# Last feed-forward block: the third group's down projection by seven block products, and the closing norm by quarters of a set

## Chip, core and metric

The kernel runs on one core of a Trainium2 chip. The metric is the device time of one execution in microseconds, as the median of several runs. TensorE is written PE, its weight loads PEld, VectorE DVE, ScalarE ACT, GpSimd POOL and SyncE SP; SP and POOL issue nearly all transfers.

## What is computed

Two encoder layers (a feed-forward block, a token mixer, a second feed-forward block) over 512 tokens and 16 meta tokens, 1024 channels wide, and a closing norm. The part that matters here is the second feed-forward block of the second layer and the norm behind it:

```python
def rmsnorm(x, g):
    xf = x.astype(jnp.float32)
    y = xf * lax.rsqrt(jnp.mean(xf * xf, axis=-1, keepdims=True) + EPS)
    return (y * g.astype(jnp.float32)).astype(x.dtype)

def swiglu(x, w_gate, w_up, w_down):
    return (jax.nn.silu(x @ w_gate) * (x @ w_up)) @ w_down
...
        h = h + 0.5 * swiglu(rmsnorm(h, norm_gains[l, 2]),
                             ffn_w_gate[l, 1], ffn_w_up[l, 1], ffn_w_down[l, 1])
    return rmsnorm(h, final_norm)[:, N_META:]
```

The hidden width is 2816, the model width 1024.

## The kernel before

Channels lie on the 128 partitions, tokens along the free dimension; `hall` holds the 8 channel chunks of `h`. In the last block only the 512 real tokens are live. Every f32 operand is cut into a rounded part (`hi`) and the rest (`lo`), and each product is three matmuls: hi·hi, hi·lo, lo·hi. ACT makes the hi part of a weight block (line 310, tile `whi`), DVE the lo part (line 311, tile `wlo`); both have four buffers.

A feed-forward block is named by layer and place: (0,0), (0,1), (1,0), (1,1). It walks over 11 pairs of hidden chunks in groups of 4, 4 and 3 pairs. For a pair, gate and up come from seven block products instead of eight (a scheme of Strassen's kind): weights and tokens are each cut in two, the seven products "1" to "7" use sums and differences of the blocks (line 621, 24 matmuls of 256 or 264 tokens each). A group's down projection goes by seven block products too where the group is "fast" (`fast_down`, line 745): the 1024 output channels are taken as two sets `dq` of 512, the products of one set have 2 x 3 x n matmuls (n pairs in the group, so 18 in the third group). A set's result has four quarters, two chunks of channels (`m`) by one half of the tokens (`q`). Product "1" alone opens an accumulator X, "6", "7" and "4" are added to it in turn; "2" opens Y; "5" opens Z and "3" is added to it. After each product DVE adds the accumulator to a quarter of `h` (line 753), before the next one may add to the same accumulator. The quarters of a set are finished by "2", "3", "7" and "4".

In blocks (0,0) and (1,0) all three groups are fast; in (0,1) and (1,1) the third is not: its down projection goes chunk by chunk of `h` (`down`, line 488), six hidden chunks for each of eight output chunks, 512 tokens at a time, and for the last three chunks of (1,1) 256 at a time (`ending`, from line 1277): first token half, then second, so that the first half's mean of squares, root and output pieces run beside the second half's products.

Weight blocks that are sums (s3 = 21 - 11, s4, and the sums for "5" and "6") are made by transfers that add into memory in SBUF (`add`, line 224, issued by POOL), by DVE, or by ACT, which negates a block first (lines 219 and 277). Plain blocks are loaded by SP (line 214), slabs of ordinary weights too (line 287). `fetch` runs 9 blocks ahead, `make` 3 or 4 ahead of the product that uses a block.

The order of the instructions on each engine is set by a scheduler from the order of the code and its dependencies; each engine takes its own list in that order. The order of the products of a third fast group is the list `CLOSING`: set 1 "1", 0 "6", 1 "2", 0 "7", 0 "3", 0 "4", 1 "5", 1 "6", 1 "7", 1 "3", 1 "4"; set 0's "1", "5" and "2" stand ahead of it.

Of the kernel before, what the change touches and what calls it, by code (L numbers as in the profile page):

```python
# [39 lines left out]


GROUPS = (4, 4, 3)
ALL_FAST = [(0, 0), (1, 0)]
LAST = [sum(GROUPS[: g + 1]) - 1 for g in range(len(GROUPS))]
QUADS = 2
LATE = 5
# [1 line left out]
OPENING = ((0, 0), 0), ((0, 0), 1)  # L48
AB = (1, 0, 1, 0, 0, 0, 1, 1, 1, 1, 1)
PACE = 0  # L50
CLOSING = tuple(zip((1, 0, 1, 0, 0, 0, 1, 1, 1, 1, 1), "16273456734"))
PLACE = {p: i for i, p in enumerate("1256743")}
DIRECT = {"1": "11", "2": "12", "4": "22"}
# [6 lines left out]
def ffn_steps(f):  # L60
# [3 lines left out]
    for g, n in enumerate(GROUPS):  # L64
# [122 lines left out]
class Weights:  # L187
# [3 lines left out]
    def __init__(self, tc, raw, hi, lo, wts, win):  # L191
# [12 lines left out]
        self.behind = None  # L204
# [45 lines left out]
    def sums(self, f, i, product, w):  # L250
# [44 lines left out]
    def make(self, upto):  # L295
        nc = self.nc
        while self.made < min(upto, len(self.loads)):
# [14 lines left out]
            self.got[s] = (hi, lo)  # L312
            self.got.pop(s - 12, None)
            self.made += 1
            if not isinstance(load, int) and load[2] in "126":
# [36 lines left out]
def build(tc, ctx, xt, wts, win, par, w2, const, umask, out):  # L352
# [243 lines left out]
    def ffn(l, f, norm, done, following):  # L596
# [94 lines left out]
        def operand(g, c, ks=None):  # L691
# [1 line left out]
            ks = ks or slice(0, GROUPS[g])  # L693
            src = raw[g][{"1": 0, "2": 2, "5": 0, "6": 0, "7": 1, "3": 3, "4": 2}[c]]
            if (g, c) not in sets:
                tag = "c" if c in "56" else "g"
# [15 lines left out]
        def operands_of(g, ks, order):  # L712
            for c in order:
                if c == "5":
                    difference(g, 0, 1, 0, ks)
                operand(g, c, ks)

        def operands_behind(g, dq, c):
            if (dq, c) == (1, "1"):
                difference(g, 1, 1, 3)  # L720
                operand(g, "7")
            elif (dq, c) == (1, "2"):
                operand(g, "3")
                difference(g, 2, 2, 0)
                operand(g, "4")

        def fast_down(g, dq, c, part):
# [22 lines left out]
            for m, q in {"1": [(0, 0)], "2": [(0, 0)], "5": [(1, 1)], "6": [(0, 1)], "3": [(0, 1)], "7": [(1, 1)],  # L750
                         "4": [(1, 0)]}[c]:
                to = hall[:, 4 * dq + 2 * m : 4 * dq + 2 * m + 2, q * w : (q + 1) * w]
                V.tensor_tensor(to, to, acc, ALU.add)  # L753
            if g == len(GROUPS) - 1:
# [522 lines left out]
    def finish_chunk(c):  # L1277
        fin.square(c)
        gain(c, slice(0, SEQ))

    def ending(sums, operand, rs):

        table("abs_reciprocal_sqrt_and_small")
# [150 lines left out]
```

## Time and profile before

| | us |
|---|---|
| median of 3 runs (2187.23 to 2188.65) | 2187.77 |
| the profiled execution | 2187.4 |
| its span, first to last instruction | 2185.6 |
| PE busy | 2149.1 (98%) |
| DVE busy | 1802.6 (82%) |
| ACT busy | 1245.9 (57%) |
| POOL busy | 119.0 (5%) |

A row of the chain of waits gives start and length and what ran; a row of the timeline adds, in brackets, the idle time of the engine ahead of it and what ended it. A row of transfers gives tiles, issuing queue, count, size and the time from issue to landing. `x24` counts instructions.

### The profile page before, as it was taken

The numbers are of one execution on the slowest core, as the hardware profiler recorded it, in microseconds if no ns is written. First come the engines' busy times: TensorE is split into PE (matmuls) and PEld (weight loads), VectorE is DVE, ScalarE is ACT, GpSimd is POOL, SyncE is SP. The second block draws the span as 40 slices with busy tenths as digits, with TensorE's granted clock in tenths as the row PEclk, the third lists the DMA queues.
The fourth block names the chain that finished last, engine by engine and source line by source line (L and its number), as shares of the span: only waits on it lengthen the run. The fifth ranks groups of instructions, "written<-read, shape, count | busy, mean of one in ns | idle before, by whom it ended". The sixth has DMA issues, their size and how long they took to land.

```text
span 2185.6 us, 40161 instructions
## 1 busy us (share of the span) xinstructions
PE 2149.1 (98%) x16434; PEld 2056.1 (94%) x16434; DVE 1802.6 (82%) x2751; ACT 1245.9 (57%) x1844; POOL 119.0 (5%) x140
## 2 busy tenths in 40 slices
PE   7999999999999999999999999999999999999998
PEld 7999999989999999999999999988788888999997
DVE  8887979776976689888789979797779767997986
ACT  8545556444784556454575455574557836554544
POOL 1100000000000000010010000000000001000100
PEclk9999999999999999999999999999999999999999
DMA  9866755212113467676567667553121146775751
GB/s 286 218 195 182 202 154 139 82 51 76 49 40 123 130 177 180 202 185 183 167 162 187 199 181 204 153 140 97 49 78 49 49 135 152 199 204 178 196 162 68
DMA packets 91223, 320.32 MB, mean 147 GB/s; under 512 B 10144, under 2 KB 12576, under 8 KB 91040
## 3 DMA queue, kind: packets, MB, share of 16 engines
q1 hardware_dynamic: 70048, 246.58, 33.9%
q0 software_dynamic: 19584, 69.21, 17.6%
q8 instruction: 129, 2.11, 0.4%
q10 hardware_dynamic: 1408, 1.97, 0.3%
q14 instruction: 54, 0.44, 0.1%
HBM read 294.65 MB, written 2.10 MB: 136 GB/s over the span
## 4 chain that ended last, share of the span: by engine, by line
PE 83%; DVE 9%; ACT 4%; DMA 2%; issue 2%; SPq 0%; DVEq 0%; ACTq 0%
PE ss L621 36%; PE mm L488 15%; PE ss L745 14%; PE ss L488 7%; DVE wlo L311 3%; PE sm L488 2%; DMA w<-win 2%; PE sm L1125 1%; PE ss L1100 1%; ACT whi L310 1%; PE ss L494 1%; DVE h L753 1%; PE sm L1141 1%; PE ss L1101 1%; PE sm L1142 1%
## 5 line engine op out<-in xcount | busy, mean ns | idle before, releaser
L621 PE MATMUL ss<-xc,whi 128*128 128x264 f32 (+1 forms) x4928 | 903.1, 285 | 11.3 <-ACT whi L310 7.4
L621 PEld LDWEIGHTS ss<-xc,whi 128*128 128x128 f32 x4928 | 764.5, 189 | 14.9 <-ACT whi L310 8.0
L621 PE MATMUL ss<-xc,wlo 128*128 128x264 f32 (+1 forms) x2464 | 700.6, 285 | 4.0 <-DVE wlo L311 4.0
L311 DVE TENSOR_TENSOR wlo<-w,whi 128x1024 fp32r<-128x1024 f32 (+2 forms) x355 | 423.7, 1200 | 66.7 <-ACT whi L310 66.3
L621 PEld LDWEIGHTS ss<-xc,wlo 128*128 128x128 f32 x2464 | 465.0, 189 | 5.9 <-DVE wlo L311 5.9
L310 ACT CAST whi<-w 128x1024 fp32r<-128x1024 f32 (+2 forms) x355 | 362.1, 1036 | 169.3 <-PE ss L621 80.1
L488 PE MATMUL mm<-x,whi 128*128 128x264 f32 (+1 forms) x1712 | 385.5, 315 | 0.0
L488 PEld LDWEIGHTS mm<-x,whi 128*128 128x128 f32 x1712 | 278.1, 188 | 16.3 <-issue 1.0
L745 PE MATMUL ss<-g,whi 128*128 128x264 f32 (+1 forms) x1520 | 284.3, 285 | 3.6 <-DVE h L753 1.7
L488 PE MATMUL mm<-x,wlo 128*128 128x264 f32 (+1 forms) x856 | 266.3, 316 | 0.0
L745 PEld LDWEIGHTS ss<-g,whi 128*128 128x128 f32 x1520 | 236.2, 188 | 7.5 <-DVE g L706 3.6
L745 PE MATMUL ss<-g,wlo 128*128 128x264 f32 (+1 forms) x760 | 215.2, 283 | 0.0
L625 ACT COPY c<-ss 128x528 f32<-128x528 f32 (+1 forms) x132 | 78.4, 594 | 239.0 <-PE ss L621 238.7
L310 ACT CAST whi<-raw 128x1024 fp32r<-128x1024 f32 x114 | 119.3, 1048 | 130.7 <-PE mm L488 94.2
L311 DVE TENSOR_TENSOR wlo<-raw,whi 128x1024 fp32r<-128x1024 f32 x114 | 139.0, 1220 | 57.2 <-ACT whi L310 53.2
L488 PEld LDWEIGHTS mm<-x,wlo 128*128 128x128 f32 x856 | 159.6, 188 | 8.5 <-issue 0.5
L745 PEld LDWEIGHTS ss<-g,wlo 128*128 128x128 f32 x760 | 143.0, 188 | 0.0
L224 POOL DMA_DIRECT2D w<-win x64 | 56.1, 876 | 1453.2 <-DVE t L1261 342.0
L745 PE MATMUL ss<-c,whi 128*128 128x264 f32 (+1 forms) x608 | 115.5, 285 | 0.3
L311 DVE TENSOR_TENSOR wlo<-s,whi 128x1024 fp32r<-128x1024 f32 (+1 forms) x94 | 112.2, 1195 | 1.6 <-ACT whi L310 1.4
L467 ACT ACTIVATE c<-c 128x528 f32<-128x528 f32 (+1 forms) x88 | 56.5, 642 | 98.5 <-DVE c L671 98.4
L488 PE MATMUL ss<-g,whi 128*128 128x264 f32 (+2 forms) x516 | 103.6, 310 | 0.0
(270 smaller groups left out, 3379.1 us busy)
## 6 DMA issues: line engine op xcount, KB each, us to landing
w<-win SPq DMA_DIRECT2D x333, 512.0 KB, 4.4
raw<-wts SPq DMA_DIRECT2D x114, 512.0 KB, 3.3
w<-win POOLq DMA_DIRECT2D x60, 512.0 KB, 7.5
s<-win POOLq DMA_DIRECT2D x26, 512.0 KB, 7.5
w<-s POOLq DMA_DIRECT2D x26, 512.0 KB, 6.1
w<-win SPq DMA_DIRECT2D x20, 384.0 KB, 3.6
s<-w POOLq DMA_DIRECT2D x8, 512.0 KB, 7.4
h<-xt SPq DMA_DIRECT2D x3, 528.0 KB, 6.0
```

The lines of the kernel that those rows point to most:

```text
L224: self.nc.gpsimd.dma_start(t, src, accum_op=ALU.add)
L310: nc.scalar.copy(hi[:, cs], w[:, cs])
L311: nc.vector.tensor_tensor(lo[:, cs], w[:, cs], hi[:, cs].bitcast(F32), ALU.subtract)
L467: prev_act[0] = S.activation(*args, **kw).ins
L488: TE.matmul(acc.half[i][:width], lhs, rhs[:, acc.spans[i]], start=first, stop=last)
L494: TE.matmul(a, weights, x[:, hs], start=True, stop=True)
L621: TE.matmul(acc[:, j], a[:, j, k], b[:, at], start=bool(begin and k == 0 and i == 0), stop=k == len(x) - 1 and i == 2, skip_group_check=no ...
L625: W.behind = S.copy(part(st, q), acc).ins
L745: closing[0] = TE.matmul(acc[:, j], a[:, j, k], xs[b][:, k], start=bool(begin and k == 0 and i == 0), stop=k == n - 1 and i == 2, skip_gro ...
L753: V.tensor_tensor(to, to, acc, ALU.add)
L1100: TE.matmul(s[:n, i, :HF], lhs, kh[:, hs], start=True, stop=False)
L1101: TE.matmul(s[:n, i, :HF], lhs, kl[:, hs], start=False, stop=True)
```

## The change

Block (1,1) joins the list `ALL_FAST`, so its third group's down projection goes by seven block products for each of the two sets. The order of its last eleven products is a list of its own, `FINAL_CLOSING`. The chunkwise closing of that block (`ending`) is no longer reached; as soon as a quarter of a set is finished, `quarter_done` scales it, squares it, sums the squares per token half and multiplies it with the gain. The second token half's four quarters are finished first; its mean, root and four output pieces are to go while the first half's last quarters are made. One weight sum (the "3" of set 1) is made by DVE from a block that is loaded a second time, instead of by an adding transfer. Of the code:

```diff
-ALL_FAST = [(0, 0), (1, 0)]
+ALL_FAST = [(0, 0), (1, 0), (1, 1)]
...
+FINAL = (DEPTH - 1, 1)
+FINAL_CLOSING = ((1, "1"), (0, "6"), (0, "3"), (1, "6"), (0, "7"), (1, "5"), (1, "7"), (1, "3"), (0, "4"), (1, "2"), (1, "4"))
...
-                    turns = [("S", g, dq, c, 3) for dq, c in CLOSING]
+                    turns = [("S", g, dq, c, 3) for dq, c in (FINAL_CLOSING if f == FINAL else CLOSING)]
...
+        elif product == "5" and self.behind_sum and f == FINAL:
+            s4, s2, key = self.behind_sum
+            V.tensor_tensor(s4, s2, s4, ALU.subtract)
+            got[key], self.behind_sum = s4, None
+        elif product == "6" and f == FINAL and i == NOP - 1:
+            s4 = self.block(f, i, "12", self.long, "wsa")
+            self.behind_sum = s4, w, (f, i, "3")
...
         def operands_behind(g, dq, c):
+            if final(g):
+                if (dq, c) == (1, "1"):
+                    difference(g, 1, 1, 3)
+                    operand(g, "3")
+                    operand(g, "7")
+                    difference(g, 2, 2, 0)
+                elif (dq, c) == (1, "5"):
+                    operand(g, "4")
+                return
...
+            if final(g):
+                if c in "2374":
+                    quarter_done(dq, *{"2": (0, 0), "3": (0, 1), "7": (1, 1), "4": (1, 0)}[c], rs)
...
+    def quarter_done(dq, m, q, rs):
+
+        half = slice(q * SEQ // 2, (q + 1) * SEQ // 2)
+        c = 4 * dq + 2 * m
+        x2 = hall[:, c : c + 2, half]
+        left[q] -= 1
...
+        V.scalar_tensor_tensor(x2, x2, -0.25, rs[:, half].unsqueeze(1).broadcast_to([P, 2, SEQ // 2]), ALU.mult, ALU.mult)
+        sq = v2(slot("t")[:, :SEQ])
+        S.activation(sq, x2, AF.Square)
+        if q not in acc:
+            acc[q] = sq
+        elif left[q] or q:
+            V.tensor_tensor(acc[q], acc[q], sq, ALU.add)
+        for i in range(2):
+            gain(c + i, half)
+        for _ in range(2 if len(waiting) > 2 else 1):
+            if waiting:
+                leave2(*waiting.pop(0))
+        if left[q] == 0:
+            t = pair(q == 1)[:, 0, : SEQ // 2]
+            parts = [acc[q][:, 0], acc[q][:, 1]] + ([sq[:, 0], sq[:, 1]] if q == 0 else [])
+            for i, p in enumerate(parts):
+                TE.matmul(t, o1024, p, start=i == 0, stop=i == len(parts) - 1)
...
+            S.activation(y, t, AF.Abs_reciprocal_sqrt, bias=eps, scale=1.0)
+            S.activation(u, y, AF.Square)
+            V.scalar_tensor_tensor(u, t, EPS, u, ALU.add, ALU.mult)
+            V.scalar_tensor_tensor(y, u, 3.0, y, ALU.subtract, ALU.mult)
...
+    def leave2(q, c, y, n):
+        half = slice(q * SEQ // 2, (q + 1) * SEQ // 2)
+        x2 = hall[:, c : c + n, half]
+        V.scalar_tensor_tensor(x2, x2, -0.5, y.unsqueeze(1).broadcast_to([P, n, SEQ // 2]), ALU.mult, ALU.mult)
+        (S if q == 0 and c % 4 == 0 else nc.sync).dma_start(out[:, c : c + n, half], x2)
```

Up to the last three pairs of this block the lists of all engines stay as they were. Line numbers grow: in the changed kernel hi and lo weight parts are lines 319 and 320, gate and up products 630, fast down products 766, additions to `h` 774.

On ACT, the stretch just ahead of the last group's down products read before (a semaphore named DMASW belongs to a transfer issued by POOL, DMAHW to one by SP):

```order
L310 CAST whi_24674<-raw_24479 128x1024 [waits DMAHW4_49,DVE_49]
L310 CAST whi_24710<-raw_24517 128x1024 [waits DMAHW5_49,PE_49]
L310 CAST whi_24747<-raw_24554 128x1024 [waits DMAHW6_49,DVE_49,PE_49]
L467 ACTIVATE c_24408<-c_24408 128x512 [waits DVE_49]
L310 CAST whi_24751<-raw_24586 128x1024 [waits DMAHW7_49,PE_49,Activation_49]
```

Now this stands there, around the second to fifth of the eleven turns (`w_11_15` and `s_11_15` are weights of set 0, `w_11_16` and `s_11_16` of set 1; 24766 serves (0,"6"), 24827 (0,"3"), 24862 (1,"6"), 24889 (0,"7"); c_24793, g_24853 and g_24857 are the hidden operands of "6", "3" and "7"):

```order
L319 CAST whi_24766<-w_11_15_24413 128x768 [waits DMASW2_49,PE_49]
L319 CAST whi_24827<-s_11_15_24770 128x768 [waits DMASW4_49,PE_49]
L712 CAST c_24793<-g_24277 128x256 [waits DVE_49]
L472 ACT_TABLE_LOAD
L319 CAST whi_24862<-w_11_16_24553 128x768 [waits DMASW6_49,PE_49]
L709 ACTIVATE g_24853<-g_24280 128x768 [waits DVE_49]
L319 CAST whi_24889<-s_11_15_24631 128x768 [waits DMASW0_49,PE_49]
L712 CAST g_24857<-g_24278 128x768 [waits PE_49]
```

The casts of plain loaded slabs have gone; casts of weights that adding transfers make stand among the casts of the operands.

On DVE, the same place held this before:

```order
L684 TENSOR_TENSOR c_24407<-c_24407 128x512
L477 TENSOR_TENSOR g_24742<-c_24407,g_24742 128x512
L311 TENSOR_TENSOR wlo_24781<-raw_24621,whi_24780 128x1024
L587 TENSOR_TENSOR h<-h,ss_24612 128x512
L587 TENSOR_TENSOR h<-h,ss_24661 128x512
```

And now (ss_24693 is set 0's accumulator X, ss_24744 its Z, ss_24765 its Y):

```order
L320 TENSOR_TENSOR wlo_24767<-w_11_15_24413,whi_24766 128x768
L715 TENSOR_TENSOR c_24794<-g_24277,c_24793 128x256
L774 TENSOR_TENSOR h<-h,ss_24693 128x2x256
L774 TENSOR_TENSOR h<-h,ss_24744 128x2x256
L710 SCALAR_TENSOR_TENSOR g_24854<-g_24280,g_24853 128x768
L774 TENSOR_TENSOR h<-h,ss_24765 128x2x256
L715 TENSOR_TENSOR g_24858<-g_24278,g_24857 128x768
L1316 SCALAR_TENSOR_TENSOR h<-h,rs_21346 128x2x256
L320 TENSOR_TENSOR wlo_24828<-s_11_15_24770,whi_24827 128x768
```

The low part of (0,"3")'s weights, the last row, stands behind the operands of "3" and "7", which take their hi parts from ACT.

At the end of PE's list the first half's mean stood between the second half's products before:

```order
L1295 MATMUL ss_24929<-t_24792,const 128x256
L488 MATMUL ss_24856<-g_24314,whi_24747 128x256 x2
L488 MATMUL ss_24856<-g_24314,wlo_24748 128x256
L488 MATMUL ss_24856<-g_24279,whi_24747 128x256 x2
L488 MATMUL ss_24856<-g_24279,wlo_24748 128x256
L488 MATMUL ss_24856<-g_24547,whi_24751 128x256 x2
L488 MATMUL ss_24856<-g_24547,wlo_24752 128x256
L1300 MATMUL ss_24929<-t_24926,const 128x256
```

Now its list ends so (ss_25058 is the second token half's mean, ss_25153 the first's):

```order
L766 MATMUL ss_24826<-c_24997,whi_25066 128x256
L766 MATMUL ss_24826<-c_24996,wlo_25067 128x256
L1332 MATMUL ss_25058<-t_24915,const 128x256 x2
L1332 MATMUL ss_25153<-t_24822,const 128x256 x2
L1332 MATMUL ss_25153<-t_25147,const 128x256 x2
```

Both means stand behind the last product.

More of the change, by code (lines that the diff above doesn't have):

```diff
@@ L203, in __init__ @@
         self.pos = 0
-        self.behind = None
+        self.behind = self.behind_sum = None
     def dram(self, f, i, name):
@@ L314, in make @@
             self.made += 1
-            if not isinstance(load, int) and load[2] in "126":
+            if not isinstance(load, int) and load[2] in "1265":
                 self.sums(*load, w)
@@ L695, in operand @@
             if (g, c) not in sets:
-                tag = "c" if c in "56" else "g"
+                tag = "c" if c in "56" or final(g) and c == "4" else "g"
                 sets[g, c] = [quarter(tag, F32R) for _ in range(2)]
@@ L716, in operands_of, with final @@
                 operand(g, c, ks)
+        def final(g):
+            return done is None and g == len(GROUPS) - 1
         def operands_behind(g, dq, c):
+            if final(g):
[7 more added lines that the diff above has]
+                return
             if (dq, c) == (1, "1"):
@@ L753, in fast_down @@
                 V.tensor_tensor(to, to, acc, ALU.add)
-            if g == len(GROUPS) - 1:
+            if final(g):
+                if c in "2374":
+                    quarter_done(dq, *{"2": (0, 0), "3": (0, 1), "7": (1, 1), "4": (1, 0)}[c], rs)
+            elif g == len(GROUPS) - 1:
                 if c in "34":
@@ L1279, in finish_chunk @@
         gain(c, slice(0, SEQ))
+    left = {0: 4, 1: 4}
+    acc, factor_of, ms_of, waiting = {}, {}, {}, []
+    def quarter_done(dq, m, q, rs):
[3 more added lines that the diff above has]
+        left[q] -= 1
+        if len(acc) == 0:
+            table("abs_reciprocal_sqrt_and_small")
+        V.scalar_tensor_tensor(x2, x2, -0.25, rs[:, half].unsqueeze(1).broadcast_to([P, 2, SEQ // 2]), ALU.mult, ALU.mult)
[15 more added lines that the diff above has]
+                TE.matmul(t, o1024, p, start=i == 0, stop=i == len(parts) - 1)
+            y, u = slot("t")[:, : SEQ // 2], sq[:, 0]
+            S.activation(y, t, AF.Abs_reciprocal_sqrt, bias=eps, scale=1.0)
+            S.activation(u, y, AF.Square)
+            V.scalar_tensor_tensor(u, t, EPS, u, ALU.add, ALU.mult)
+            V.scalar_tensor_tensor(y, u, 3.0, y, ALU.subtract, ALU.mult)
+            pieces = [(q, c, y, 2) for c in (0, 2, 4, 6)] if q else [(q, c, y, 2) for c in (0, 2, 4)] + [(q, c, y, 1) for c in (6, 7)]
+            if q:
+                waiting.extend(pieces)
+            else:
+                for p in pieces:
+                    leave2(*p)
+    def leave2(q, c, y, n):
[3 more added lines that the diff above has]
+        (S if q == 0 and c % 4 == 0 else nc.sync).dma_start(out[:, c : c + n, half], x2)
     def ending(sums, operand, rs):
```

## The prediction

> **What bounds the kernel now.** I read the share of the engines first (TensorE, PE, ahead of all), then the chain of waits over the last 94 us, since the change touches nothing earlier, and then the stretch of the trace where the same product scheme already runs in a third group. The shares, and the chain of waits of the last stretch, start and length in us, then what ran:
>
> ```profile
> PE 2149.1 (98%) x16434; PEld 2056.1 (94%) x16434; DVE 1802.6 (82%) x2751; ACT 1245.9 (57%) x1844; POOL 119.0 (5%) x140
> ...
> 2131.84 2.76 PE ss L488 x12
> 2134.61 2.83 PE ss L621 x24
> ...
> 2167.40 0.57 PE ss L1295 x2
> ...
> 2169.52 5.25 PE ss L488 x45
> ...
> 2174.79 0.43 DVE h L1291
> ...
> 2175.71 0.42 ACT t L1296
> 2176.18 0.71 PE ss L1300 x2
> 2176.91 0.48 ACT t L1306
> 2177.42 0.42 ACT t L1307
> 2177.87 0.44 DVE t L1308
> 2178.33 0.44 DVE t L1309
> 2178.79 0.69 DVE h L1313
> ```
>
> PE alone carries it from 2131.84 (first down product of the last group) to 2174.77, then a serial chain of 4.0 us (add, scale, square, mean, root) leads to the first finished piece at 2178.79, and 6.8 us of pieces and stores lead to the span's end at 2185.6. Two rows by stretch (busy time and instruction count of PE, PEld, DVE, ACT, POOL; clock; transfers): the stretch that is replaced, and the third group of block (1,0), which does now what the change makes the last group do.
>
> ```profile
> 2131.84:2174.77 42.93, 42.93 (x276) 38.83 (x275) 30.41 (x50) 22.60 (x35) 0.00 (x0) 1.00 0.13 44
> 1421.06:1457.09 36.03, 34.76 (x277) 33.95 (x277) 35.14 (x53) 25.40 (x36) 4.38 (x5) 1.00 0.64 165
> ```
>
> In the stretch that goes, VectorE (DVE) has 12.5 us to spare, transfers are at 0.13 and PE is never idle. In the model stretch DVE is busy 35.14 of 36.03 us and transfers are at 0.64. So the change takes work from an engine with no rival and gives it to one that is full.
>
> **The change part by part.** PE first. Down products before: 90 matmuls of 512 tokens and 108 of 256, as the tiles' view has them (66 plus 132 instructions; 30+60 wide, 36+72 narrow).
>
> ```profile
> L488 PE MATMUL ss<-g,whi x132: 276/281/468, 2131.7 to 2174.4; 128*128 128x256 f32 x72, 128*128 128x512 f32 x60
> L488 PE MATMUL ss<-g,wlo x66: 276/281/398, 2132.1 to 2174.5; 128*128 128x256 f32 x36, 128*128 128x512 f32 x30
> ```
>
> A wide one takes 2.76/12 = 0.230 us, a narrow one 5.25/45 = 0.117, together 33.3 us. After: 14 products of 18 narrow ones, 252 x 0.1177 (2.83/24) = 29.7. Saved: 3.7. The 1.1 us of the two mean matmuls in mid-stream (0.57 and 0.49) leave the stream too, for its end. From 2131.84 the new stream holds 72 gate and up matmuls and 252 down ones, 324 x 0.1177 = 38.1 us: without a wait it ends at 2169.95, **4.8 us earlier**.
>
> Now the waits. The model stretch maps onto the new one at a fixed distance: there product "4" of the last pair ends at 1425.44, here at 2131.84 + 84 x 0.1177 = 2141.73 (24+24+12+24 matmuls stand before that end), so +716.3. The stretch lost time too:
>
> ```profile
> 1425.44 7.37 PE ss L745 x60
> ...
> 1454.66 2.42 PE ss L745 x18
> ```
>
> Ten turns of 18 from 1432.80 to 1457.08 took 24.3 us, where ten times 7.37/60 x 18 = 2.2 is 22.1: 2.2 us lost, with the DVE full. What differs here is the order: set 0's product "3" comes third, set 1's "6" fourth, where the model has them fifth and eighth. Their weights are sums that transfers build. Issue by GpSimd (POOL) in the model, in this order: s3 of set 1, s4 of set 0, the "5" sum of set 1, the "6" sum of set 1; and the landings of the first, second and fourth (the view of transfers, last number us from issue to landing):
>
> ```profile
> 1422.96 0.87 POOL L224 DMA_DIRECT2D s<-win  x1 [9.37 <-DVE wlo L311]
> 1423.69 1.03 POOL L224 DMA_DIRECT2D s<-w  x1
> ...
> 1431.54 0.88 POOL L224 DMA_DIRECT2D w<-s  x1 [4.94 <-issue]
> s<-win POOLq DMA_DIRECT2D x1, 384.0 KB, 7.9
> s<-w POOLq DMA_DIRECT2D x1, 384.0 KB, 9.4
> w<-s POOLq DMA_DIRECT2D x1, 384.0 KB, 5.9
> ```
>
> The order of loads and issues up to here is the model's, so I shift them by 716.3: the weights of (0,"3") are there at 1423.69+9.4+716.3 = 2149.4, those of (1,"6") at 1431.54+5.9+716.3 = 2153.7 (its issue waits for s3's landing, 1430.9). ScalarE (ACT) rounds both in the order shown ahead, and what stands behind each waits. The durations: two 768-wide casts 1.57, so 0.75 apart; a 256-wide cast 0.41, 0.30 apart; the negated operand of "3" 0.86; on DVE an h addition 0.62 to the next start for 528 tokens, so 0.61 for 512, a 768-wide operand 0.89 and a low part 0.87:
>
> ```profile
> 1428.99 1.57 ACT L310 CAST whi<-w 128x768 fp32r<-128x768 f32 x2 [0.65 <-PE ss L745]
> 1426.31 0.41 ACT L703 CAST c<-g 128x264 fp32r<-128x264 f32 x1
> 1435.69 0.86 ACT L700 ACTIVATE g<-g 128x792 fp32r<-128x792 f32 x1
> 1438.32 0.70 DVE L753 TENSOR_TENSOR h<-h,ss 128x528 f32<-128x528 f32 x1
> 1438.94 0.97 DVE L701 SCALAR_TENSOR_TENSOR g<-g,g 128x792 fp32r<-128x792 f32 x1
> 1439.83 0.97 DVE L710 TENSOR_TENSOR g<-g,g 128x792 f32<-128x792 f32 x1
> 1440.72 0.95 DVE L311 TENSOR_TENSOR wlo<-w,whi 128x768 fp32r<-128x768 f32 x1
> ```
>
> Step by step. PE ends (1,"1") at 2148.7. ACT casts (0,"3") 2149.4 to 2150.15, and only then the last piece of the operand of "6" (0.30), so that its low part on DVE ends at 2150.85 and the h addition that frees (0,"6")'s accumulator at 2151.5: first wait, 2.8 us. PE runs (0,"6") to 2153.6. ACT stands at the cast of (1,"6") until 2153.7, ends it at 2154.5 and makes the operand of "3" by 2155.35. DVE, which waits there, makes its low part (2156.2), adds to h (2156.8), makes the operand of "7" (2157.7), scales (2158.3) and only then makes (0,"3")'s low weights: 2159.2. PE needs them from the third matmul on, has 16 left, 1.9 us, and ends the turn at 2161.1 instead of 2146.6 + 3 x 2.12 = 2152.96: **8.1 us lost**. Over the next eight turns (8 x 2.12 = 16.95) DVE has, until the last low weights are there, 8 low parts (7.0), 8 h additions, 3 scalings and 1 sum of squares (12 x 0.61 = 7.3), one weight difference and one operand (0.87 and 0.89): 16.0 us, ending at 2175.2, and PE asks at 2175.9. That is even, with no cover left, and no gain back. Products end at 2178.05.
>
> [...] No row of this case shows an ACT instruction that passed another.
>
> **The close.** Before, 4.0 us lead from the last product to the first piece. After, the second half's mean stands behind the last product on PE, and on ACT its root stands ahead of three of the first half's squares. Two f32 means at 0.57, about 1.3 us with the last of the sum of squares, to 2179.4; root 0.48; a 512 square, 0.55 apart; the square of the root 0.42; two gains 0.9; two more squares 1.1: 2182.9. DVE adds, and PE has four f32 means, 4 x 0.57: 2185.3. Root, square and two corrections 0.48+0.42+0.44+0.44: 2187.1, 9.0 us behind the last product. The second half's four pieces (4 x 0.61) fit in the wait for these. The rest, five pieces and their stores on the same queues, I take as before: 6.8. So **15.8 for 10.8: 5.0 us more**. The square and gain rows this uses:
>
> ```profile
> 2155.56 1.24 ACT L522 ACTIVATE t<-h 128x512 f32<-128x512 f32 x2 [3.21 <-DVE h L592]
> 2172.42 0.51 ACT L1275 ACTIVATE h<-h,par 128x256 f32<-128x256 f32 x1
> ```
>
> The sum: -4.8 + 8.1 + 5.0 = +8.3, span 2193.9. The profiled execution took 2187.4 for its span of 2185.6, 0.4 below the median 2187.77, so I add the difference to the median: **2196**.
>
> What the trace doesn't show is how those transfers land in the new company. The lower bound are the same three kinds where little else moved: 6.4, 4.9 and 5.1, by which (1,"6") is there at 2151.4, 2.3 us sooner, and the time is 2193.8. The upper bound is the slowest of that stretch, 9.7, for the last of them: 3.8 us later, 2199.9. I take the model's own landings, since order and load are its own.
>
> ```profile
> s<-win POOLq DMA_DIRECT2D x1, 384.0 KB, 6.4
> s<-w POOLq DMA_DIRECT2D x1, 384.0 KB, 4.9
> w<-s POOLq DMA_DIRECT2D x1, 384.0 KB, 5.1
> w<-win POOLq DMA_DIRECT2D x1, 384.0 KB, 9.7
> ```
>
> **The rivals.** First: the sums land before ACT asks, and only DVE's own queue counts. Then ACT is done with the operand of "3" at 2150.8, (0,"3")'s low weights come at 2154.65 and the turn ends at 2156.6, 4.5 us sooner: +3.8, 2191.6. For it: they land 5 to 10 us after issue, and POOL might issue sooner. Against: even the fastest rows give 2151.4 for (1,"6"). [...]
>
> Second, the other side: no wait of weight, and the close grows only by longer instructions. Product stream to 2169.95, and from there the 4.0 us with 512-wide add, scale and square (0.26, 0.25, 0.21 more) and one more mean (0.5): 1.2 more. That is -3.6, 2184.2; with the model's own loss of 2.2, 2186.4. It decides if ACT has the operand of "3" by 2150 and the second half's mean is formed before the last turn ends. For it: the model, with the same 14 products, lost 2.2 us only. Against: the order rows, which put that mean behind the last product and the cast ahead of the operand.
>
> Third: a new late transfer. The "12" block of set 1 is loaded a second time, into the buffer that (0,"3") frees at 2159.2, and DVE subtracts it at 2164.2. A load alone takes 2.9, in company 8.0; at 8.0 DVE comes 3.0 us late, of which 0.7 is slack: 2198.3.
>
> ```profile
> w<-win SPq DMA_DIRECT2D x1, 384.0 KB, 2.9
> w<-win SPq DMA_DIRECT2D x1, 384.0 KB, 8.0
> ```
>
> **How the numbers follow.** Forecast 0.60 (own range 2193 to 2199), first rival 0.18, second 0.10, third 0.12. A measurement of this kernel tells about 0.2%, 4.4 us, from no change: slower begins at 2192.15, faster ends at 2183.4. The first rival, centred 0.5 below that edge, gives 0.11 to the same and 0.07 to slower; the second 0.07 and 0.03 to faster. Slower 0.79, same 0.18, faster 0.03. The range is 2190 to 2199.5: it leaves out the second rival and a tail above.
>
> **What would show it.** ACT idle ahead of the casts of (0,"3") and (1,"6"), ended by transfers, about 2149 and 2153; PE idle some 2.8 us ahead of the second turn and some 5 in the third; DVE full from there to the end; products ending near 2178; the mean of the second half behind them, and the first piece of the first half 9 us later. Wrong if those casts find their weights there (first rival), if PE is not idle in the third turn, or if the end comes less than 13 us behind the last product.

## The result, and the profile after

The changed kernel takes 2198.56 us (median of 4 runs, 2198.02 to 2199.61) where the kernel before, in runs beside it, took 2187.50 (2186.79 to 2188.65): ratio 1.0050, 95% interval 1.0037 to 1.0063, so it is slower by 11.1 us. The forecast was 2196.0, the range 2190 to 2199.5. The profiled execution took 2198.67 us for a span of 2196.7; before it was 2187.4 for 2185.6, so 11.1 us more in the span as well.

The stretch of the last down products, from the profile's view by stretch (length, then busy time and count of PE, PEld, DVE, ACT and POOL, clock, share of the transfer engines, GB/s). Before, the stretch from 2131.84 held 42.93 us, all of it PE work.

```profile
2131.84:2180.74 48.90, 41.96 (x327) 40.97 (x326) 41.57 (x64) 28.70 (x45) 3.51 (x4) 0.93 0.37 88
```

PE has less work (41.96 us), and stands idle for 7 us. It also ran at a mean clock of 0.93, where it had 1.00. VectorE is busy for 41.57 us against 30.41 before. The chain of waits shows the order in which this came about (start, length, what ran):

```profile
2140.97 8.08 DMA s<-w
...
2149.13 0.83 ACT whi L319
...
2150.64 0.69 DVE h L774
...
2151.47 2.37 PE ss L766 x18
...
2154.58 0.84 ACT g L709
...
2158.47 0.88 DVE wlo L320
...
2159.40 21.35 PE ss L766 x160
2180.74 0.88 PE ss L1332 x4
...
2181.64 0.47 ACT t L1334
...
2185.13 3.54 PE ss L1332 x8
...
2190.56 0.69 DVE h L1348
```

Read from the top: the transfer that builds set 0's weights of "3" lands at 2149.05, ScalarE rounds them at 2149.13, VectorE comes to the addition that frees the accumulator at 2150.64, and the second turn starts at 2151.47. The third turn gets its low weights at 2159.35. From 2159.40 PE runs through to the last product at 2180.74, which was 2174.77 before. The first finished piece of the first half comes at 2190.56, 9.8 us later (4.0 before), and 6.1 us more lead to the end (6.8 before). So 6.0 us of the 11.1 lie ahead of the last product's end and 5.1 behind it. ScalarE's own rows show the two stops (in brackets the idle time ahead and what the profile takes for its end):

```profile
2149.13 0.83 ACT L319 CAST whi<-s 128x768 fp32r<-128x768 f32 x1 [2.91 <-DMA s<-w]
2149.87 0.40 ACT L712 CAST c<-g 128x256 fp32r<-128x256 f32 x1
2150.29 1.28 ACT L472 ACT_TABLE_LOAD   x1
2153.84 0.83 ACT L319 CAST whi<-w 128x768 fp32r<-128x768 f32 x1 [2.27 <-PE ss L766]
```

For the second stop the profile names PE, whose second turn ended at that moment (2153.84). The transfer that makes these weights, issued at 2147.49, landed 6.3 us later, at the same moment. Which of the two it was is asked of an experiment below.

What PE waited for from 2100 on (us in all, times, longest), and the granted clock (last but two) in steps of 2 us:

```profile
PE ss L1332 <- DVE t L1322: 3.5, 1, 3.5
PE ss L766 <- DVE wlo L320: 2.6, 1, 2.6
PE ss L766 <- DVE h L774: 1.9, 1, 1.9
PE ss L766 <- ACT g L709: 1.6, 1, 1.6
PE ss L766 <- DVE g L710: 0.6, 1, 0.6
```

```profile
2154.00:2156.00 2.00, 0.39 (x1) 0.19 (x1) 0.55 (x1) 2.00 (x3) 0.00 (x0) 1.00 0.00 0
2156.00:2158.00 2.00, 0.39 (x1) 0.19 (x1) 2.00 (x4) 1.60 (x3) 0.00 (x0) 0.89 0.00 0
2158.00:2160.00 2.00, 0.60 (x3) 0.60 (x4) 2.00 (x4) 1.46 (x3) 0.00 (x0) 0.50 0.00 0
2160.00:2162.00 2.00, 2.00 (x11) 2.00 (x11) 2.00 (x3) 0.08 (x1) 0.00 (x0) 0.50 0.63 193
2162.00:2164.00 2.00, 2.00 (x11) 2.00 (x11) 1.06 (x3) 0.83 (x1) 0.00 (x0) 0.50 0.05 12
2164.00:2166.00 2.00, 2.00 (x18) 2.00 (x17) 2.00 (x3) 0.17 (x1) 0.00 (x0) 0.90 0.00 0
```

This is what the prediction had not foreseen. Between 2153.84 and 2159.40 PE ran two matmuls, and by 2158 its clock had fallen to a half. At 2160 to 2164 it is busy all the time, yet does 11 matmuls in 2 us where at full clock it does 17. The 160 matmuls from 2159.40 took 21.35 us; at 0.1177 each they would have taken 18.8.

### The profile page after: what moved, and what is told of

The parts are those of the page before. It is cut to its first block, busy times and chain, and to the rows that moved or that the text cites. A ratio compares the mean times of both kernels' runs of the same rounds, so it can differ in the third digit from the quotient of the medians.

```text
span 2196.7 us, 40363 instructions
## 1 busy us (share of the span) xinstructions
PE 2152.1 (98%) x16492; PEld 2061.9 (94%) x16492; DVE 1817.6 (83%) x2771; ACT 1255.6 (57%) x1862; POOL 125.1 (6%) x147
## 4 chain that ended last, share of the span: by engine, by line
PE 83%; DVE 9%; ACT 4%; DMA 2%; issue 2%; SPq 0%; DVEq 0%; POOL 0%; ACTq 0%; POOLq 0%
PE ss L630 37%; PE ss L766 16%; PE mm L497 15%; PE ss L497 5%; DVE wlo L320 2%; PE sm L497 2%; DMA w<-win 1%; PE sm L1149 1%; PE ss L1124 1%; ACT whi L319 1%; DVE h L774 1%; PE ss L503 1%; PE sm L1165 1%; PE ss L1125 1%; PE sm L1166 1%
## 5 line engine op out<-in xcount | busy, mean ns | idle before, releaser
L320 DVE TENSOR_TENSOR wlo<-w,whi 128x1024 fp32r<-128x1024 f32 (+2 forms) x366 | 435.6, 1197 | 69.5 <-ACT whi L319 68.9
L319 ACT CAST whi<-w 128x1024 fp32r<-128x1024 f32 (+2 forms) x366 | 371.1, 1030 | 175.7 <-PE ss L630 82.3
L766 PE MATMUL ss<-g,whi 128*128 128x264 f32 (+1 forms) x1616 | 303.4, 285 | 6.1 <-ACT g L709 2.3
L766 PEld LDWEIGHTS ss<-g,whi 128*128 128x128 f32 x1616 | 252.1, 189 | 10.4 <-DVE g L715 3.8
L766 PE MATMUL ss<-g,wlo 128*128 128x264 f32 (+1 forms) x808 | 229.6, 284 | 2.6 <-DVE wlo L320 2.6
L319 ACT CAST whi<-raw 128x1024 fp32r<-128x1024 f32 x108 | 113.0, 1048 | 123.4 <-PE mm L497 93.8
L320 DVE TENSOR_TENSOR wlo<-raw,whi 128x1024 fp32r<-128x1024 f32 x108 | 131.9, 1222 | 53.5 <-ACT whi L319 49.5
L766 PEld LDWEIGHTS ss<-g,wlo 128*128 128x128 f32 x808 | 152.8, 189 | 2.8 <-DVE wlo L320 2.8
L766 PE MATMUL ss<-c,whi 128*128 128x264 f32 (+1 forms) x680 | 129.4, 286 | 2.3 <-DVE h L774 1.9
L774 DVE TENSOR_TENSOR h<-h,ss 128x528 f32<-128x528 f32 (+1 forms) x154 | 106.2, 699 | 8.0 <-PE ss L766 7.3
```

What stands on the lines that cost most here:

```text
L319: nc.scalar.copy(hi[:, cs], w[:, cs])
L320: nc.vector.tensor_tensor(lo[:, cs], w[:, cs], hi[:, cs].bitcast(F32), ALU.subtract)
L766: closing[0] = TE.matmul(acc[:, j], a[:, j, k], xs[b][:, k], start=bool(begin and k == 0 and i == 0), stop=k == n - 1 and i == 2, skip_gro ...
```

## The experiments

Each kernel ran beside the kernel before on the same chip. The times come from four sessions, in which the kernel before had medians of 2188.51 (e1 to e4), 2187.88 (e5 to e8), 2189.24 (e9 to e11) and 2188.19 (e12), so the table compares what each takes over the kernel before.

| run | what it is | us over before | ratio, 95% interval |
|---|---|---|---|
| e5 | the change, unaltered | 11.45 | 1.0052 (1.0039 to 1.0065) |
| e1 | without the adding transfers | 2.92 | 1.0014 (1.0006 to 1.0023) |
| e2 | without one of them | 7.86 | 1.0040 (1.0027 to 1.0052) |
| e3 | matmuls without use in the idle time | 9.22 | 1.0046 (1.0032 to 1.0060) |
| e4 | late sums asked for later, a store missing | 5.62 | 1.0028 (1.0017 to 1.0039) |
| e6 | the same, all stores | 5.04 | 1.0022 (1.0012 to 1.0031) |
| e7 | e6 and a relieved close | 4.08 | 1.0018 (1.0009 to 1.0027) |
| e8 | the change without the second half's mean | 10.55 | 1.0046 (1.0032 to 1.0060) |
| e9 | e7, means behind the last product | 1.89 | 1.0008 (0.9999 to 1.0017) |
| e10 | the change, low weights first | 8.06 | 1.0038 (1.0025 to 1.0050) |
| e11 | e10 and the close of e9 | 6.98 | 1.0037 (1.0023 to 1.0051) |
| e12 | e9, its sums on VectorE | 4.35 | 1.0019 (1.0010 to 1.0028) |

**The yardstick (e5).** No edit.

> The changed kernel unaltered, on the chip and among the runs of the others, as their yardstick, and as a second look at the granted clock. Both theories: 11 us over the kernel before (within 1.5 us). Theory on the clock: with the idle time of about 8 us out of 11 before the third turn the clock falls to about a half again; if it stays at 1.00 here with the same idle time, the 2.5 us belong to chance and not to the change.

Measured: 2199.33 us, 11.45 over. PE's idle times in this profile lie otherwise (3.3 us in one piece ahead of the second turn, 2.4 in the third), and the clock fell sooner, but it fell again: 0.50 from 2154 to 2164. So the half clock comes with this order of turns, and not by the chance of one execution.

**Are the transfers the cause? (e1)** The edit leaves them out in the last group:

```diff
-    def add(self, t, src):
+    def add(self, t, src, f=None, i=0):
+        if f == FINAL and i >= NOP - QUADS:
+            return
         self.nc.gpsimd.dma_start(t, src, accum_op=ALU.add)
```

> Leaves out every adding transfer of the last block's third group (six per pair of sets), so the sums of weight blocks there are incomplete; all instructions of TensorE, ScalarE and VectorE stay. Theory (late landings hold ScalarE at two casts, VectorE queues behind, TensorE idles about 6 us and is then granted half clock): the idle time ahead of both casts goes, only VectorE's full queue is left (the first rival's 4.4 us less), and the granted clock stays near 1.00 after the second turn (2.5 us less): 2191.7, between 2190.5 and 2193; last product near 2174 to 2175 of the span. Rival (VectorE's queue alone holds TensorE, the transfers are covered by it): within 1 us of 2198.6, and the clock falls as before.

Measured: 2191.43 us. PE's waits in the products, and the stretch that ran at half clock in the change:

```profile
PE ss L768 <- DVE wlo L322: 1.7, 1, 1.7
PE ss L768 <- DVE h L776: 0.7, 1, 0.7
```

```profile
2159.30:2164.00 4.70, 4.70 (x42) 4.70 (x41) 4.70 (x8) 4.14 (x8) 0.00 (x0) 1.00 0.01 2
```

Two waits of 2.4 us are left of four of 6.7, PE stays at full clock, and the last product ended at 2172.3 of the span, sooner than the 2174 to 2175 forecast; 1.2 us of that is this execution's own, which came to the last feed-forward block earlier. The transfers, and what follows from them, are worth 8.5 us (11.45 less 2.92; the intervals lie apart). That is the price of all of them together with their load: the six plain loads from 2130 us on landed in 3.3 us at the median here, 4.5 in the change. The rival falls.

**Which one ended ScalarE's second stop? (e2)**

```diff
-                self.add(got[f, i, "6"], got[f, i, "7"])
+                if f != FINAL or i != NOP - 1:
+                    self.add(got[f, i, "6"], got[f, i, "7"])
```

> Leaves out one adding transfer alone, the one that makes set 1's block for product 6 (its operand is then only one of the two summands). It tells what ended ScalarE's wait at the cast of that block: the profile names TensorE (the end of the second turn), the theory says this transfer, issued 2147.49 and landed 6.3 us later. Theory: the cast runs about 2.2 us sooner, the second turn's low weights (VectorE) are ready near 2157.1 instead of 2159.4: 2.3 us less, 2196.3, and up to 2.5 us more off if the shorter idle time keeps the clock at full: 2193.8. Rival (the cast waits for TensorE's turn as the profile has it): 2198.6 within 0.7 us, the cast still at 2153.8.

Measured: 2196.37 us. The profiled execution, about 1.3 us later in all its times than that of the change, shows the table load, the cast behind it, and the start of PE's second turn:

```profile
2152.87 1.28 ACT L473 ACT_TABLE_LOAD   x1
2154.05 0.77 PE L767 MATMUL ss<-c,whi 128*128 128x256 f32 x2 [3.29 <-DVE h L775]
2154.16 0.83 ACT L320 CAST whi<-w 128x768 fp32r<-128x768 f32 x1
```

The cast follows the table load at once, without idle time, while PE has only begun the turn whose end the profile had named. So the stop was the transfer's, and PE's end at the same moment was chance. In e5 and e3, where the two moments lie apart, the profile itself names the transfer (for 1.56 and 1.96 us of idle time). The median agrees with 2196.3, though its interval overlaps that of e5. This execution, the slowest of the five, does not show the 2.2 us: by the same distance of 1.3 us its cast came 1.0 us sooner, as the weights of (0,"3"), one stop earlier, landed 9.4 us after issue where the change had 8.1. The further 2.5 us did not come: PE still waited 3.3 us in one piece ahead of the second turn, and the clock went to 0.50.

**Does idle time cause the half clock? (e3)**

```diff
             st["w"].pop(c)
+            if final(g) and (dq, c) == (0, "6"):
+                for _ in range(20):
+                    TE.matmul(st["X"][:, 0, w : 2 * w], hi[:, 0, 0], xs[0][:, 0], start=True, stop=True)
```

> Adds 20 matmuls of 256 columns without use, into free columns of a bank, between the first two turns, where TensorE otherwise idles; about 2.4 us of work. Theory (the half clock from 2159 to 2164 follows from the idle time before it): the clock stays near 1.00, the turn of set 0's product 3 runs at 0.118 us a matmul instead of 0.214, 2.5 us less: 2196.1 (1.7 us less if the fill is too short to hold it all). Rival (the clock falls for another reason): 2198.6 within 0.7 us, the granted clock 0.50 in the same place.

The fill writes into a bank that holds open sums of set 0 and changes them. Measured: 2197.73 us, 9.22 over. The chain's row for the products, and the clock in steps:

```profile
2161.57 19.12 PE ss L766 x160
```

```profile
2154.00:2156.00 2.00, 2.00 (x10) 2.00 (x11) 0.40 (x1) 0.05 (x1) 0.00 (x0) 0.50 0.08 17
2156.00:2158.00 2.00, 2.00 (x13) 2.00 (x13) 0.38 (x1) 1.99 (x3) 0.00 (x0) 0.65 0.00 0
2158.00:2160.00 2.00, 2.00 (x19) 2.00 (x18) 2.00 (x4) 1.05 (x2) 0.00 (x0) 1.00 0.00 0
```

In this execution PE idled 3.2 us ahead of the second turn and ran that turn at half clock; so the expectation that the fill would keep the clock up throughout did not come true. The clock was full again at 2157.4, within that turn and 0.3 us ahead of the fill. The fill (2157.7 to 2160.2) then stood where the change waits, only 1.1 us of idle time was left in the third turn, the clock stayed, and the same 160 matmuls took 19.12 us instead of 21.35: 2.2 of the 2.5 us. The run e8 below is the counterpart without a fill: its clock was full again at 2158.4 as well, PE then idled 0.5 and 2.6 us, and at 2161.8 it fell once more. The time alone does not tell the two theories apart, as its interval overlaps that of e5; the late transfer landed some 0.7 us later here and took back a part. The rows decide. The other runs agree: the six with no idle piece over 1.8 us among the turns (e1, e4, e6, e7, e9, e12) stayed at 1.00 there; those with one of 2.45 us or more (the change, e2, e3, e5, e8, e10, e11) all fell to a half. What decides it more closely is in the last section.

**Asking later (e4, e6).** In place of the third and fourth turn stand (1,"2") and (0,"7"), which need no late sum, and the operand of "7" is formed before that of "3". In e6 the last quarter's call hands out all waiting pieces:

```diff
-FINAL_CLOSING = ((1, "1"), (0, "6"), (0, "3"), (1, "6"), (0, "7"), (1, "5"), (1, "7"), (1, "3"), (0, "4"), (1, "2"), (1, "4"))
+FINAL_CLOSING = ((1, "1"), (0, "6"), (1, "2"), (0, "7"), (0, "3"), (1, "6"), (1, "5"), (1, "7"), (1, "3"), (0, "4"), (1, "4"))
...
-        for _ in range(2 if len(waiting) > 2 else 1):
+        for _ in range(4 if left[0] == 0 else 2 if len(waiting) > 2 else 1):
```

> The same work, the eleven turns in another order: set 0's product 3 and set 1's product 6, whose weight sums land late, are asked for two turns later, and products 2 of set 1 and 7 of set 0 go ahead of them. Theory: the casts no longer wait for transfers, TensorE idles less than 2 us in all among the turns and the clock stays: 6 to 8 us less, 2190.6 to 2192.6; what is left over the kernel before (2187.5) is the longer close, about 5 us less the gain in the product stream. Rival (VectorE's queue holds the turns whatever their order): 2196 to 2198.6.

> The order of turns of the run before it of that kind (set 0's product 3 and set 1's product 6 asked for later), with all pieces stored: that run left out one of the nine stores, a 256 KB piece of the second half. Theory: the waits for transfers stay gone, 5.5 to 7 us over the kernel before, and nearly all of it lies behind the last product (close 16 us for 10.8). Rival: the missing piece made the gain, 9 us or more over.

Measured: 2194.13 us (5.62 over) and 2192.92 (5.04 over). e4 lies 1.5 us above what was expected of it, e6 half a microsecond below; the missing store made no gain. In e6 PE's waits in the products are 2.8 us, none over 1.1, and the clock is full:

```profile
PE ss L766 <- DVE h L774: 1.7, 2, 1.0
PE ss L766 <- DVE wlo L320: 1.1, 1, 1.1
```

Its last product ended at about 2174.4 of the span (2174.77 in the kernel before), and 16.4 us of close follow. So with the late transfers out of the way, what the change costs is its close. The 4.8 us that the product stream should gain are still not there: the 2.8 us of waits that are left end with VectorE, which is busy without a break over most of the turns (24.0 of the 24.0 us from 2146 to 2170).

**What is late in VectorE's queue (e10).** Order of turns, transfers and close are those of the change:

```diff
                     operand(g, "3")
-                    operand(g, "7")
-                    difference(g, 2, 2, 0)
+                elif (dq, c) == (0, "6"):
+                    operand(g, "7")
+                    difference(g, 2, 2, 0)
```

> The changed kernel with its own order of turns, its transfers and its close; only the operand of product 7 is formed one turn later, by which the low weights of set 0's product 3 come ahead of the negated operand, of that operand and of a scaling in VectorE's queue. Theory (VectorE, first in first out, held the low weights some 3 us behind the operand of product 3): third turn 2.5 to 3 us sooner, 6.5 to 9 us over the kernel before instead of 11.4; the waits at the two casts stay. Rival (the transfers alone set that turn): less than 1 us less.

Measured: 2197.30 us, 8.06 over. ScalarE's stop and PE's third turn:

```profile
2154.88 0.83 ACT L319 CAST whi<-w 128x768 fp32r<-128x768 f32 x1 [1.85 <-DMA w<-s]
2157.50 0.58 PE L767 MATMUL ss<-g,whi 128*128 128x256 f32 x1 [0.17 <-DVE g L710]
```

The stop is still there, and here the profile names the transfer. From that cast to PE's going on in the third turn there are 2.6 us instead of 5.6 (2153.84 to 2159.40): the turn came 2.9 us sooner, as expected, and the time is 3.4 us less. The intervals of the two times overlap, but the rows show the step. So of what the late transfers cost, some 3 us were the place of the low weights in VectorE's queue.

**The close (e8, e7, e9, e11, e12).** e8 leaves out the second half's mean:

```diff
-        if left[q] == 0:
+        if left[q] == 0 and q:
+            waiting.extend((q, c, rs[:, half], 2) for c in (0, 2, 4, 6))
+        elif left[q] == 0:
             t = pair(q == 1)[:, 0, : SEQ // 2]
```

> The changed kernel without the mean of the second half and without its root and corrections; its pieces are scaled by another factor that is there (so the second half of the output is not the reference's). Theory (that mean and its root stand ahead of the first half's squares and cost about 1.3 us there): the first half's first piece comes 1.2 to 2 us sooner behind the last product, 1.2 to 2 us less than the changed kernel. Rival (only longer instructions make the close longer): less than 0.6 us less.

Measured: 2198.43 us, 0.9 less than e5 by what each takes over its kernel before, between theory and rival and with overlapping intervals. VectorE, PE's mean and the first piece:

```profile
2182.44 0.69 DVE L1350 SCALAR_TENSOR_TENSOR h<-h,rs 128x512 f32<-128x512 f32 x1
2183.04 0.69 DVE L774 TENSOR_TENSOR h<-h,ss 128x512 f32<-128x512 f32 x1
...
2184.84 0.69 DVE L1350 SCALAR_TENSOR_TENSOR h<-h,rs 128x512 f32<-128x512 f32 x1
2185.44 0.68 DVE L774 TENSOR_TENSOR h<-h,ss 128x512 f32<-128x512 f32 x1
...
2186.88 3.75 PE L1334 MATMUL ss<-t,const 128*128 128x256 f32 x8 [4.13 <-DVE t L1322]
...
2192.54 2.57 DVE L1350 SCALAR_TENSOR_TENSOR h<-h,t 128x512 f32<-128x512 f32 x5
```

The last product ended at 2182.75, and the first piece came at 2192.54: 9.8 us, just what the change has. Without the mean to wait for, the second half's pieces (L1350) went ahead of the last quarters' additions (L774) in VectorE's queue, and the time freed on ScalarE was spent there. This run does not give the mean's price; it shows that VectorE's queue sets this part.

e7 and e9 take e6 and relieve that queue; e9 also ties the means behind the last product, where e7's scheduler had put two of them among the last turns:

```diff
-        elif left[q] or q:
-            V.tensor_tensor(acc[q], acc[q], sq, ALU.add)
+        elif left[q] > 1 or q:
+            nc.gpsimd.tensor_tensor(acc[q], acc[q], sq, ALU.add)
+        elif left[q]:
+            factor_of[0] = sq
...
+            parts = [z[:, i] for z in factor_of[q] for i in range(2)]
+            with after(closing[0]):
+                for i, p in enumerate(parts):
+                    TE.matmul(t, o1024, p, start=i == 0, stop=i == len(parts) - 1)
```

> The same order, and the close relieved: four sums of squares go from VectorE to GpSimd, the next-to-last quarter's squares go to the mean directly (six mean matmuls for the first half in place of four) instead of being added first, and the gains of the first half's last two quarters are formed after the squares. Theory (in the last 25 us VectorE's full queue sets the products and the close): 3 to 5 us less than the order alone, 1 to 3.5 us over the kernel before. Rival (the close is set by the matmuls in full float and by ScalarE, not by VectorE): within 1 us of the order alone.

> As the run with the relieved close, but all mean matmuls stand behind the last product on TensorE (there they stood in the middle of products and TensorE waited 3.3 us for GpSimd and ScalarE in front of them), and the gains follow the squares. Theory (close set by VectorE's queue and by the mean's matmuls behind the last square): 2 to 3 us less than that run, 1 to 2 us over the kernel before, within 0.2% of it. Rival (GpSimd's sums, 1.75 us each, come late wherever the means stand): no less than that run's 4.1 us over.

Measured: 2191.96 us (4.08 over; 1.0 less than e6, so the rival's figure) and 2191.13 (1.89 over, as expected, and within 0.2% of the kernel before). In e7 the way from the last product to the first piece fell to 5.4 us (2176.74 to 2182.15), so the relief works, but two means stood among the turns, where PE waited 2.1 us for GpSimd's sums (of the 3.3 us that the expectation of e9 names, 1.2 lay behind the last product). In e9 that way is 7.8 us (2176.35 to 2184.15), behind products without those waits. The same close on the order of the change (e11) and e9's with its sums on VectorE again (e12, one word: nc.gpsimd to V):

> The two together: low weights first, with the order of turns of the change, and the close relieved and behind the last product. Theory: the gains add, about 4 us less than low weights first alone, 2.5 to 5 us over the kernel before; the half clock, if TensorE still idles over 3 us at one place, keeps it there. Rival (relieving the close gives nothing where the waits for transfers stay): within 1 us of low weights first alone.

> The run with the means behind the last product once more, its sums of squares back on VectorE (0.69 us each) from GpSimd (1.2 to 2.0 us each, and VectorE's 512-wide scalings took up to 1.78 us for 0.69 while GpSimd added). Theory now: GpSimd's help costs VectorE as much as it saves, and its sums come late for the mean (1.1 us of TensorE's wait); back on VectorE within 1 us of that run, 1 to 3 us over the kernel before. Rival (VectorE's queue is what counts, each sum 0.69): 2 to 3 us more than that run.

Measured: 2196.22 us (6.98 over) and 2192.54 (4.35 over). In e11 the gains do not add: 1.1 us less than e10, the rival's side. GpSimd's sums in e11, and VectorE's rows beside them:

```profile
2169.68 1.98 POOL L1323 TENSOR_TENSOR t<-t,t 128x512 f32<-128x512 f32 x1 [21.12 <-ACT t L1319]
2173.89 1.81 POOL L1323 TENSOR_TENSOR t<-t,t 128x512 f32<-128x512 f32 x1 [2.23 <-ACT t L1319]
```

```profile
2172.40 0.68 DVE L1317 SCALAR_TENSOR_TENSOR h<-h,rs 128x512 f32<-128x512 f32 x1
...
2174.47 1.78 DVE L1317 SCALAR_TENSOR_TENSOR h<-h,rs 128x512 f32<-128x512 f32 x1
```

The scaling that starts beside GpSimd's second sum takes 1.78 us, the same scaling alone 0.68. In all, five rows of VectorE beside the four sums took 3.1 us longer than such rows alone, where four sums on VectorE at 0.69 us would be 2.8: what VectorE was to save is lost there. e12 then lies 2.5 us above e9, the rival's side, but the intervals overlap (e9 up to 1.0017, e12 from 1.0010). Whether GpSimd's help is worth its price here stays open. No version beat the kernel before; e9 comes level with it.

## Why the prediction was right, and where it was short

**Step 1, the product stream without waits (-4.8): held, worked back from the trace.** No run shows the stream without a wait. Taking from 2180.74 PE's waits up to there (1.9, 1.6, 0.6, 2.6 and 0.2 us), the 2.5 us of the half clock and some 0.8 us of slower matmuls in the second and third turn (mostly the two single ones ahead of a wait) leaves 2170.5, where the step had 2169.95.

**Step 2, the waits (+8.1): right in its mechanism and nearly to the tenth in its places.** Forecast and measured: weights of (0,"3") 2149.4 and 2149.05; second turn from 2151.5 and 2151.47; the cast of (1,"6") free at 2153.7 and 2153.84; low weights of (0,"3") at 2159.2 and 2159.35. That they meet so closely is partly luck. The transfer for (0,"3") was issued 1.0 us later than worked out (2140.97 for 2140.0) and landed 1.3 us faster (8.1 us for 9.4); in e5, the same kernel, it took 9.4, the second turn began at 2153.13 and the third went on at 2160.35. e1 and e2 show that the transfers held those casts, and e10 that VectorE's order made 3 us of it. No row here shows an instruction of ScalarE or VectorE that passed another; in the change the rows of both begin in the order of their lists: the negated operand of "3" at 2154.58, behind the cast of (1,"6") at 2153.84, and the low weights of (0,"3") at 2158.39, behind the operand of "7" at 2156.92 and a scaling at 2157.79. The end of the turn, 2161.1, was then 2 us too early, and the products' end (2178.05 against 2180.74) 2.7 us. What failed there is the term for the 16 matmuls left in that turn and those behind it: they were priced at full clock, 0.118 us each, although the step itself had PE idle for 2.8 and some 5 us ahead of them, and ran at 0.214 until 2164.4. Of the 2.7 us the half clock is 2.5.

**Step 3, the close (+5.0): right in sum (5.1), not in its parts.** The way to the first piece is 9.8 us for 9.0, the rest 6.1 for 6.8, so the sum came right by two errors that cancel. The four means of the first half were priced 2.3 us and took 3.54, at a clock of 0.62 between 2186 and 2189. The reason given, that the second half's mean and its root stand in the way, was not borne out: without them (e8) the way is as long, since VectorE's queue fills it. What they cost by themselves stays open.

**The sum.** +8.3 was forecast for the span, +11.1 measured, 2.8 more. The half clock in the products (2.5) and the slower means (1.2) would make that 3.7; the shorter stretch of pieces and stores (0.7) and small differences took back the rest. The range reached up to 2199.5 for later landings and for the third rival (2198.3). Neither made the time, so that 2198.56 lies inside it is owed to room left for other causes.

**The rivals.** The first (2191.6, no wait for transfers) is what e1 makes: 2191.43, or 2.9 us over the kernel before where the rival had 3.8; its price was about right and its condition not met. The second (the close grows only by longer instructions) needed a mean formed before the last turn ended; it stood behind it, and the close grew by 5.1 us. The third did not come: the block loaded a second time landed 4.7 us after its issue at 2159.4, ahead of VectorE's subtraction at 2165.29.

**Where the expected gain went.** The change saves PE 4.8 us that e6, with the late transfers out of the way and at full clock, still does not show: 2.8 us of it are PE's waits for VectorE there. The change moves the last stretch from an engine with nothing beside it to one that is full (VectorE is busy for 19.90 of the 21.34 us from 2159.40), and the close adds VectorE's work where nothing hides it.

## What to carry to other kernels

Before a faster scheme replaces a slower one at the end of a program, look at what the slower one leaves idle: here it hid VectorE and asked for no built weights. When a forecast leaves TensorE idle for half of some 3.4 us or more (1.8 us of 3.41 was the least that did it in these runs), price the matmuls behind it at half clock; here it lasted 3.4 to 13.7 us among the products, longer where more idle time followed. And when the profile names one releaser and another event falls on the same moment, take one of them away before believing it.

## What was not expected of the hardware

**The granted clock falls after short idle pieces.** In e11 PE idled 2.45 us up to 2151.78, and the clock, 1.00 from 2150 to 2152, was 0.60 from 2152 to 2154 and full again from 2156. In the change it was at a half from 2157.6 to 2164.4, 5 us into busy work. Among the turns the half clock lasted 3.41 us or a multiple of it wherever it came (3.4 in e3 and e11 and twice in e8, 6.8 in the change and e10, 10.2 in e2, 13.7 in e5), so idle time is counted here in steps of that length. Two such steps, from e5, ending where its clock fell, and from e1, whose clock did not fall (the steps of e1 are counted back from its next fall, at 2176.62):

```profile
2148.66:2152.07 3.41, 1.19 (x11) 0.99 (x9) 0.96 (x2) 1.26 (x3) 0.83 (x1) 1.00 1.08 262
2149.32:2152.73 3.41, 2.16 (x19) 1.95 (x17) 3.41 (x6) 2.42 (x4) 0.00 (x0) 1.00 0.00 0
```

PE was idle for 2.2 us of the first and 1.25 of the second. Counted so over all these profiles from 1900 us of the span on, every step at full clock with 1.8 us or more of idle time was followed by half clock (the least was in e4, behind its products), and none with up to 1.4. Once at a half, a step with up to 0.5 us of idle time brought the clock back, and one with 0.7 or more kept it down. So what fits all runs is the idle share of a step, some half of it, and not the longest piece: in the change the fall came 0.7 us into the longest piece, and e1's piece of 1.7 us was cut in two by the end of a step. Where the steps begin differs from execution to execution (the first fall came at 2157.6 in the change and at 2152.1 in e5, the same kernel), so the same idle time can cost more or less.

**VectorE's rows can take longer beside GpSimd's.** 0.68 us became 1.78 in e11, and GpSimd's sums took 1.26 to 1.98. Not every row was slowed: of the additions to `h`, whose second input is an accumulator that TensorE fills, the one beside the first sum (it started at 2170.42) took 0.69 and the one beside the last (2179.40) 0.68, as elsewhere. What makes the difference was not shown.

**Adding transfers are dear.** Between 2138 and 2166 of the changed kernel the queues read so (packets, MB, share of 16 engines' time):

```profile
q0 software_dynamic: 576, 1.57, 29.8%
q1 hardware_dynamic: 730, 1.98, 24.5%
```

The first are GpSimd's four that add, the second mostly plain loads that SyncE issues. Per MB the adding ones held the engines for 19.0% of that time, the plain ones for 12.4%, half as much again, and they landed 6.3 to 8.8 us after issue while those engines were full (share 1.07 from 2149 to 2152). Whether the adding or the other queue makes the price, no run tells.
